# The first half of the output weights, loaded and split at a later place of the program

## The chip, the cores and the metric

One Trainium2 chip, of which the kernel uses one core. The metric is the device time of one execution in microseconds (us); lower is better. Four compute engines work beside each other, each through its own instructions in a fixed order: PE multiplies matrices, ACT (ScalarE) and DVE (VectorE) work elementwise and read PE's results, POOL (GpSimd) works elementwise on SBUF. Transfers are started by SP (most) and POOL, each again in a fixed order, and carried by 16 DMA engines that all share.

## The reference

A decoder layer on x of 1024 tokens by 1024 channels, all in float32. Cut to what matters here:

```
proj = rms_norm(x) @ w_in                      # split into q, kv, gates ...
y_a  = nsa_mixer(q, kv, ...)                   # attention: 8 heads, 3 branches
y_a  = (y_a * silu(g_nsa)) @ w_proj_a          # 512 -> 1024
y_b  = rglru_mixer(u, ...)                     # recurrent branch
y_b  = (y_b * silu(g_lru)) @ w_proj_b          # 512 -> 1024
m    = sigmoid(gate_a) * y_a + sigmoid(gate_b) * y_b
out  = x + m @ w_out                           # 1024 -> 1024
```

## The kernel before

Every float32 operand of a large product is split into a high part and a rest, and one product becomes three matmuls (`mm3`, lines 170 to 172). So each weight tile is loaded into `w_raw` (line 176; two buffers, 512 KB a load), copied to its high part on ACT, and subtracted on DVE or POOL to get the rest (lines 184, 185; for `w_out` lines 1014, 1015). A `w_raw` buffer is free again when the subtraction is done.

The program is written as a list of work, and a scheduler fixes the order on every engine when it is built: work that stands earlier in the text has precedence, work that is ready fills gaps. `attention()` writes the attention and, between its steps, pieces of the side work (`fill`). When attention is written out, the rest of the side work follows, in a tail in which all products go to the four PSUM buffers `ps_s` and all loads of a gate go to a ring of eight SBUF buffers, four cut from a tile named `bias` and four from `kTs`. The tail has these parts:

- The second branch's products with `w_pb`: eleven of them fall into the tail, each of 12 matmuls over 512 columns. A product ends with line 888 on DVE, which reads its `ps_s` buffer and a loaded gate `gb` (line 876). The result is stored to `mb` by a DMA on POOL (line 95, function `dst`), and the ring buffer is loaded again (with a gate `ga`, line 777) once that store has landed.
- `gated(1)` and `gated(0)`: the gated attention output of tokens 512 to 1023 and 0 to 511: loads of `yo` (line 761) and `gn`, lines 763 and 765 on DVE, 764 and 767 on ACT, 768 on DVE. `yo` is what attention stores (lines 709 to 711); the last of it is stored late in the tail, and two `kTs<-yo` loads wait for it.
- `merge(1)`, then `merge(0)`: eight products each with `w_pa` (four tiles), 12 matmuls a product; line 792 on DVE reads the `ps_s` buffer, then 796, 798 (ACT) and 799 make the merged tile, `big_h` or `t`.
- `out_weights(0)`, the first half of `w_out` (columns 0 to 511): four loads of 512 KB, eight ACT copies, eight DVE subtractions, into buffers that attention has given up (`p_slc`, `p_win`, `ph`, `pl`).
- The output products `ps_t` (lines 1023 on), 24 matmuls for 128 tokens by 512 columns. Those that have their merged tile and weights are put between the merge products.

A `ps_s` buffer is given to the next product only when DVE has read it, so DVE's order decides when PE may go on.

Of the kernel before, what the change touches and what calls it, by code (L numbers as in the profile page):

```python
# [73 lines left out]
def f(ap):  # L74
    return ap.bitcast(FT)


def fr(ap):
    return ap.bitcast(FR)
# [7 lines left out]
def _build(ctx, tc, A, out, dbg):  # L87
# [21 lines left out]
    @contextmanager  # L109
    def urgent(by):  # L110
        tc.cur_priority -= by
        yield
        tc.cur_priority += by
# [13 lines left out]
    def ps_f(most):  # L127

        if tail:
            return next(tail[0])()[:, 0:most]  # L130
        return (ps("ps_f", PF) if PF else ps_s())[:, 0:min(most, FW)]
# [11 lines left out]
    def ta(dt=FT):  # L143
        return K.tile([128, S], dt, name="t", bufs=NTILE)
# [4 lines left out]
    def te():  # L149
        if tail:  # L150
            return next(tail[1])
        return K.tile([128, 512], FT, name="ev", bufs=NEV)
# [4 lines left out]
    def t_st():  # L157
        return K.tile([128, 512], FT, name="st", bufs=4)
# [4 lines left out]
    def p_slc():  # L163
        return K.tile([128, 4 * WTOK], FT, name="p_slc", bufs=1)

    def p_win():
        return K.tile([128, 2560], FT, name="p_win", bufs=1)

    def mm3(o, lh, ll, rh, rl, first, last):
        T.matmul(o, lh, rh, start=first, stop=False)  # L170
        T.matmul(o, lh, rl, start=False, stop=False)  # L171
        T.matmul(o, ll, rh, start=False, stop=last)  # L172
# [354 lines left out]
    def prep_stage():  # L527
        if preps:
            try:
                next(preps[0])  # L530
            except StopIteration:
                preps.pop(0)
# [222 lines left out]
    def gated(half, y1):  # L755

        tk = slice(half * 512, (half + 1) * 512)
        ya = []
        for kc in range(4):
            yt, gt = te(), t_st()  # L760
            dma(yt, yo[2 * kc:2 * kc + 2, :, tk].rearrange("h d t -> (h d) t"))
            dma(gt, gn[kc, :, tk])
            V.scalar_tensor_tensor(out=yt, in0=yt, scalar=0.5, in1=gt, op0=OP.mult, op1=OP.mult)
            C.activation(gt, gt, AF.Tanh, scale=0.5)
            V.scalar_tensor_tensor(out=yt, in0=gt, scalar=1.0, in1=yt, op0=OP.add, op1=OP.mult)
            y2 = y1[:, kc] if y1 is not None else ta(FR)
            C.activation(y2[:, 0:512], yt, AF.Copy)
            V.tensor_tensor(out=y2[:, 512:], in0=yt, in1=f(y2[:, 0:512]), op=OP.subtract)
            ya.append(y2)
        return ya  # L770

    def merge(half, pa, m1, ya):

        tk = slice(half * 512, (half + 1) * 512)
        for m in range(8):
            gt, bt = te(), t_st()
            dma(gt, ga[m, :, tk])
            dma(bt, mb[m, :, tk])
            wh, wl = pa[m // 2]
            c = slice((m % 2) * 128, (m % 2 + 1) * 128)  # L780
            q = 0
            while q < 512:
                s = ps_f(512 - q)
                w = s.shape[-1]
                for kc in range(4):
                    mm3(s, wh[:, kc, c], wl[:, kc, c], ya[kc][:, q:q + w], ya[kc][:, 512 + q:512 + q + w],
                        kc == 0, kc == 3)
                    if kc < 3:
                        yield w * 0.00126
                tq = slice(q, q + w)  # L790
                with urgent(UPE):
                    V.scalar_tensor_tensor(out=gt[:, tq], in0=gt[:, tq], scalar=1.0, in1=s, op0=OP.add, op1=OP.mult)
                q += w
                if q < 512:
                    yield w * 0.00126
            (V if tail else G).tensor_tensor(out=gt, in0=gt, in1=bt, op=OP.add)
            mt = m1[:, m] if m1 is not None else ta(FR)
            C.activation(mt[:, 0:512], gt, AF.Copy, scale=0.5)
            V.scalar_tensor_tensor(out=mt[:, 512:], in0=gt, scalar=0.5, in1=f(mt[:, 0:512]),
                                   op0=OP.mult, op1=OP.subtract)  # L800
            mT[half, m] = mt
            yield w * 0.00126
# [111 lines left out]
    def fill(us):  # L914
        owed[0] += us
        while owed[0] > 0:
            p0 = tc.cur_priority
            tc.cur_priority = p0 + LOWP
            if LOOK and len(marks) >= LOOK:
                with tc.issue_after(marks[-LOOK]):  # L920
                    d = next(side, None)
            else:
                d = next(side, None)
            tc.cur_priority = p0 + (tc.cur_priority - p0 - LOWP if KEEPP else 0)
            if not d:
                owed[0] = 0.0
                return
            owed[0] -= d

    def attention():  # L930
        late = []

        def drain():
            if late:
                late.pop(0)()

        def prepare(*tbs):
            while any(x in tbs for x in todo):
                prep_stage()
                fill(F_PREP)  # L940

        seq = [(g,) + u for g in range(2) for u in units(g)]
        n = len(seq) // 2

        ahead = {k: [k + 1] for k in range(2 * n)}
        ahead[0] = ahead[n - 1] = []
        ahead[EARLY] += [n]
        ahead[2 * n - 1] = []
        prepare(3, 4, 5, 6, 7)
        for j in seq[0][1]():  # L950
            j()
            fill(F_Q)
        for k, (g, jobs, steps) in enumerate(seq):
            if k == n:
                drain()
                prepare(*range(NT))
            more = []
            if k == 1:
                prepare(*range(NT))
                for _ in qkv1_:  # L960
                    pass
                for j in jobs():
                    j()
                    fill(F_JOB)
                fill(F_LEAD)
            for a in ahead[k]:
                if a == n:
                    prepare(3, 4, 5, 6, 7)
                more += seq[a][1]()
            m = len(steps)  # L970
            per = (FK[k] if FK else max(F_MIN, LAT / m - 1.32)) if k else F_Q
            at = [min(m - 1, int(j * (m - 1) / max(1, len(more)))) for j in range(len(more))]
            if k > 1:
                fill(FB[k])
            for q, st in enumerate(steps):
                pvk = st()
                js = [more[j] for j in range(len(more)) if at[j] == q]
                for j in js:
                    j()
                    fill(per / len(js))  # L980
                if not js:
                    fill(per)
                drain()
                late.append(pvk)
                prep_stage()
        drain()
        wo0.extend(out_weights(0))
        r1 = K.tile([128, 4, 512], FT, name="bias")
        r2 = K.tile([128, 2, 64 + S], FT, name="kTs", bufs=1)
        ring = [r1[:, k] for k in range(4)] + [r2[:, a, c:c + 512] for a in range(2) for c in (0, 512)]  # L990
        tail.extend([itertools.cycle([ps_s] * PB[0]), itertools.cycle(ring)])
        if not pa:
            gated_y[1] = gated(1, None)
        gated_y[0] = gated(0, None)
        for _ in side:
            pass
        for _ in merge(0, pa, None, gated_y[0]):
            pass

    def out_weights(nh):  # L1000
        if nh == 0:
            ws, ww = fr(p_slc()), fr(p_win())
            wo = [(w[:, k * 1024:k * 1024 + 512], w[:, k * 1024 + 512:(k + 1) * 1024])
                  for w, n_ in ((ws, 4), (ww, 2)) for k in range(n_)]
            wo += [[K.tile([128, 512], FR, name=n_, bufs={"ph": 2, "pl": NPL}[n_]) for n_ in ("ph", "pl")] for _ in range(2)]
        else:
            w = [t_l(0, 8), t_l(1, 8)]
            wo = [(w[k // 4][:, k % 4], w[k // 4][:, 4 + k % 4]) for k in range(8)]
        for kp in range(4):
            raw = wload(A["w_out"][nh, kp])  # L1010
            for k in range(2):
                r = raw[:, k * 512:(k + 1) * 512]
                wh, wl = wo[2 * kp + k]
                C.activation(wh, r, AF.Copy)
                V.tensor_tensor(out=wl, in0=r, in1=f(wh), op=OP.subtract)
        return wo

    wo0 = []
    if True:
        attention()  # L1020
# [98 lines left out]
```

## Time and profile before

| | |
|---|---|
| median of 3 runs | 905.2 us (902.38 to 905.53) |
| the profiled execution's own time | 903.51 us |
| its span, first to last instruction | 901.7 us |
| PE busy | 872.1 us, 97% of the span |
| DVE, ACT, POOL busy | 569.1, 441.4, 298.5 us |
| DMA | 92.49 MB, mean 103 GB/s |

The profiled execution lies 1.7 us under the median. PE is busy nearly all the time, so the time is PE's work and PE's gaps. The tail runs from about 727 us to the end.

### The profile page before, as it was taken

To read this page: it belongs to the slowest core of one execution; us is meant where nothing else is said; L and a number is where in the kernel's file an instruction comes from. 1 tells how busy PE (TensorE), PEld (TensorE's weight loads), DVE (VectorE), ACT (ScalarE), POOL (GpSimd) and SP (SyncE) were. 2 spreads that over 40 slices of the span, in tenths; PEclk is the share of its full clock that TensorE was granted. 3 is DMA by queue.
4 is the path that set the end of the run, shared out by engine and by line. 5 is a ranking of instruction groups with operands and counts; after the bars stand their busy time and mean duration, and the time that the engine had idled before them with its cause. 6 is when DMAs were issued, how large, how long until landed. Compare 5 with 4: busy or idle time off the path is not lost.

```text
span 901.7 us, 15836 instructions
## 1 busy us (share of the span) xinstructions
PE 872.1 (97%) x5670; PEld 779.5 (86%) x5670; DVE 569.1 (63%) x1627; ACT 441.4 (49%) x1161; POOL 298.5 (33%) x338
## 2 busy tenths in 40 slices
PE   5999999989899999999999999999999999999998
PEld 4778888989899999999999998999998877888887
DVE  4563868897622548576577857667777886783111
ACT  7432453646423547566456757566667663331000
POOL 4032243279512435253355644233324421000000
PEclk9999999999999999999999999999999999999999
DMA  9133421202212112112122241121113369883121
GB/s 354 53 99 114 155 87 48 77 30 76 101 48 83 47 60 84 64 53 77 48 65 77 67 138 54 37 71 56 40 46 117 125 212 342 330 271 109 71 71 47
DMA packets 45519, 92.49 MB, mean 103 GB/s; under 512 B 6896, under 2 KB 12704, under 8 KB 45440
## 3 DMA queue, kind: packets, MB, share of 16 engines
q1 hardware_dynamic: 44480, 88.33, 29.3%
q0 software_dynamic: 960, 3.15, 0.9%
q8 instruction: 44, 0.72, 0.3%
q14 instruction: 35, 0.29, 0.1%
HBM read 64.15 MB, written 25.21 MB: 99 GB/s over the span
## 4 chain that ended last, share of the span: by engine, by line
PE 83%; DVE 6%; POOL 3%; DMA 3%; ACT 3%; issue 1%; SPq 0%; ACTq 0%; DVEq 0%; POOLq 0%
PE ps_f L170 10%; PE ps_f L171 9%; PE ps_f L172 9%; PE ps_s L624 7%; PE ps_s L170 7%; PE ps_s L172 7%; PE ps_s L171 7%; PE ps_t L677 6%; PE ps_t L170 4%; PE ps_t L171 4%; PE ps_t L172 4%; PE ps_o L701 3%; PE ps_o L702 3%; DVE sq L548 1%; POOL ss L193 1%
## 5 line engine op out<-in xcount | busy, mean ns | idle before, releaser
L171 PE MATMUL ps_f<-big_l,w_hi 128*128 128x256 f32 (+1 forms) x700 | 200.3, 286 | 0.0
L170 PE MATMUL ps_f<-big_h,w_hi 128*128 128x256 f32 (+1 forms) x664 | 193.8, 292 | 0.8 <-ACT ev L841 0.6
L172 PE MATMUL ps_f<-big_h,w_lo 128*128 128x256 f32 (+1 forms) x664 | 189.6, 286 | 0.0
L171 PEld LDWEIGHTS ps_f<-big_l,w_hi 128*128 128x128 f32 x700 | 131.9, 188 | 2.0
L170 PEld LDWEIGHTS ps_f<-big_h,w_hi 128*128 128x128 f32 x664 | 125.6, 189 | 4.5 <-ACT ev L841 2.0
L172 PEld LDWEIGHTS ps_f<-big_h,w_lo 128*128 128x128 f32 x664 | 125.4, 189 | 1.8 <-POOL w_lo L185 0.3
L682 DVE TENSOR_TENSOR pl<-ps_t,ph 128x512 fp32r<-128x512 f32 x132 | 90.4, 687 | 47.1 <-ACT ph L681 45.6
L185 POOL TENSOR_TENSOR w_lo<-w_raw,w_hi 128x1024 fp32r<-128x1024 f32 x32 | 77.9, 2438 | 97.6 <-ACT w_hi L184 75.0
L681 ACT ACTIVATE ph<-ps_t 128x512 fp32r<-128x512 f32 x132 | 78.1, 599 | 48.8 <-PE ps_t L677 45.5
L662 POOL TENSOR_SCALAR p_slc<-p_slc,mx,bg 128x384 f32<-128x384 f32 (+7 forms) x88 | 68.6, 785 | 90.1 <-DVE mx L661 35.3
L658 ACT ACTIVATE p_slc<-ps_s,mx 128x256 f32<-128x256 f32 (+5 forms) x128 | 68.1, 540 | 24.0 <-DVE mx L656 18.2
L171 PE MATMUL ps_s<-big_l,w_hi 128*128 128x512 f32 (+1 forms) x184 | 73.2, 398 | 0.0
L184 ACT ACTIVATE w_hi<-w_raw 128x1024 fp32r<-128x1024 f32 (+1 forms) x40 | 42.3, 1061 | 38.3 <-PE ps_f L171 17.7
L648 DVE TENSOR_REDUCE mx<-ps_s 128x1 f32<-128x256 f32 (+5 forms) x120 | 50.9, 436 | 10.7 <-PE ps_s L624 9.2
L701 PE MATMUL ps_o<-ph,t 128*128 128x512 f32 x132 | 55.7, 422 | 0.0
L170 PE MATMUL ps_s<-big_h,w_hi 128*128 128x512 f32 x136 | 54.4, 408 | 0.4 <-ACT big_h L245 0.3
L662 POOL TENSOR_SCALAR p_win<-p_win,mx,bg 128x640 f32<-128x640 f32 (+1 forms) x40 | 34.7, 869 | 59.1 <-DVE mx L661 25.0
L677 PE MATMUL ps_t<-ident_r,p_slc 128*128 128x128 f32 x336 | 54.0, 273 | 0.0
L653 DVE CUSTOM_DVE_ANT_0 ps_s<-ps_s,bias 128x256 f32<-128x256 f32 (+1 forms) x128 | 52.5, 417 | 2.3 <-POOL p_win L662 0.8
L172 PE MATMUL ps_s<-big_h,w_lo 128*128 128x512 f32 x136 | 53.4, 395 | 0.4 <-POOL w_lo L185 0.4
L624 PE MATMUL ps_s<-kTs,t 128*128 128x512 f32 (+4 forms) x224 | 53.0, 349 | 0.3 <-ACT pc L633 0.3
L702 PE MATMUL ps_o<-pl,t 128*128 128x512 f32 x132 | 53.2, 403 | 0.0
(332 smaller groups left out, 2209.9 us busy)
## 6 DMA issues: line engine op xcount, KB each, us to landing
w_raw<-in_w_in SPq DMA_DIRECT2D x30, 512.0 KB
t<-in_x SPq DMA_DIRECT2D x8, 512.0 KB
gb<-ev SPq DMA_DIRECT2D x16, 256.0 KB
ga<-ev SPq DMA_DIRECT2D x16, 256.0 KB
w_raw<-in_w_out SPq DMA_DIRECT2D x8, 512.0 KB
st<-mb SPq DMA_DIRECT2D x16, 256.0 KB
w_raw<-in_w_tok SPq DMA_DIRECT2D x6, 524.0 KB
ev<-in_cw SPq DMA_DIRECT2D x8, 256.0 KB
```

What stands on the lines that cost most here:

```text
L170: T.matmul(o, lh, rh, start=first, stop=False)
L171: T.matmul(o, lh, rl, start=False, stop=False)
L172: T.matmul(o, ll, rh, start=False, stop=last)
L185: (E or (V if tail else G)).tensor_tensor(out=lo, in0=raw, in1=f(hi), op=OP.subtract)
L624: T.matmul(s, qT[h][:, i * 128:(i + 1) * 128], rhs, start=(hl == 0), stop=(hl == 1))
L658: C.activation(p[:, h, k0:k1], sv, AF.Exp, bias=mx[:, 6:7], accum_out=mx[:, 7 + j:8 + j])
L662: G.tensor_scalar(out=p[:, h], in0=p[:, h], scalar1=mx[:, 9:10], scalar2=bg[:, g, i, 4 * (br + 1) + h:4 * (br + 1) + h + 1], op0=OP.mult, ...
L677: ins = T.transpose(pt[:, h * 128:(h + 1) * 128], p[h][:, c0:c0 + 128], ident)
L681: C.activation(ph, pt, AF.Copy)
L682: V.tensor_tensor(out=pl, in0=pt, in1=f(ph), op=OP.subtract)
L701: T.matmul(o, vf, pp[0], start=first, stop=False)
L702: T.matmul(o, vf, pp[1], start=False, stop=False)
```

## The change

The call of `out_weights(0)` moves from ahead of the ring, the gated tiles and the rest of the side work to a place behind them and ahead of `merge(0)`. Nothing is added or left out: the same four loads, eight copies, eight subtractions.

```diff
         drain()
-        wo0.extend(out_weights(0))
         r1 = K.tile([128, 4, 512], FT, name="bias")
         r2 = K.tile([128, 2, 64 + S], FT, name="kTs", bufs=1)
...
         gated_y[0] = gated(0, None)
         for _ in side:
             pass
+        wo0.extend(out_weights(0))
         for _ in merge(0, pa, None, gated_y[0]):
             pass
```

What the scheduler makes of it: until the tail, the order of every engine is as before. In the tail the four `w_pa` loads take the places of the first four `w_out` loads in the two `w_raw` buffers, and the `w_out` loads come behind. Two places follow in full.

SP's queue where the last part of `yo` is stored (`yo<-eo`) and read back (`kTs<-yo`). Before:

```order
L176 DMA w_raw_9255<-in_w_pa 128x1024
L876 DMA bias_8984<-gb_1266 128x512
L711 DMA yo_1268<-eo_8950 64x4x128
L777 DMA bias_8984<-ga_1265 128x512
L176 DMA w_raw_9261<-in_w_pa 128x1024
L777 DMA kTs_8985<-ga_1265 128x512
L761 DMA kTs_8985<-yo_1268 128x512 x2
```

And now:

```order
L876 DMA kTs_8955<-gb_1266 128x512 x2
L876 DMA bias_8954<-gb_1266 128x512
L777 DMA bias_8954<-ga_1265 128x512
L176 DMA w_raw_9237<-in_w_pa 128x1024
L711 DMA yo_1268<-eo_8950 64x4x128
L777 DMA kTs_8955<-ga_1265 128x512 x2
L761 DMA kTs_8955<-yo_1268 128x512 x2
```

Both `kTs<-gb` loads now stand behind two `bias<-gb` loads that wait for landed stores (before, one of them stood ahead of both), and the reading of `yo` now has two `kTs<-ga` loads ahead of it instead of one; each of those waits for the store of a second-branch product.

DVE's queue at the end of the second branch's products. `ps_s_9206`, `9222`, `9238` before and `ps_s_9176`, `9192`, `9208` now are the last three of them, `ps_s_9279` and `ps_s_9249` the first merge product. Before:

```order
L888 SCALAR_TENSOR_TENSOR bias_8984<-bias_8984,ps_s_9206 128x512
L185 TENSOR_TENSOR w_lo_9258<-w_raw_9255,w_hi_9257 128x1024
L888 SCALAR_TENSOR_TENSOR bias_8984<-bias_8984,ps_s_9222 128x512
L888 SCALAR_TENSOR_TENSOR bias_8984<-bias_8984,ps_s_9238 128x512
L185 TENSOR_TENSOR w_lo_9264<-w_raw_9261,w_hi_9263 128x1024
L763 SCALAR_TENSOR_TENSOR kTs_8985<-kTs_8985,st_9040 128x512
L792 SCALAR_TENSOR_TENSOR bias_8984<-bias_8984,ps_s_9279 128x512
```

And now:

```order
L888 SCALAR_TENSOR_TENSOR bias_8954<-bias_8954,ps_s_9192 128x512
L763 SCALAR_TENSOR_TENSOR kTs_8955<-kTs_8955,st_9010 128x512
L763 SCALAR_TENSOR_TENSOR kTs_8955<-kTs_8955,st_9019 128x512
L765 SCALAR_TENSOR_TENSOR kTs_8955<-st_9010,kTs_8955 128x512
L888 SCALAR_TENSOR_TENSOR bias_8954<-bias_8954,ps_s_9208 128x512
L765 SCALAR_TENSOR_TENSOR kTs_8955<-st_9019,kTs_8955 128x512
L185 TENSOR_TENSOR w_lo_9234<-w_raw_9231,w_hi_9233 128x1024
L185 TENSOR_TENSOR big_l1_9224<-w_raw_9237,big_l1_9224 128x1024
L768 TENSOR_TENSOR t_9016<-kTs_8955,t_9016 128x512
L792 SCALAR_TENSOR_TENSOR bias_8954<-bias_8954,ps_s_9249 128x512
```

Before, line 888 of the last second-branch product stood ahead of the two lines 763, which wait for the read of `yo`; now it stands behind them. By the waits in the built program, the second merge product gets its `ps_s` buffer from that line 888, and the third from line 792 of the first, which now has both `w_pa` subtractions ahead of it.

## Rows read from the trace of the kernel before

**Rows 1.** The page: PE's busy time, and its granted clock in 40 slices.

```profile
PE 872.1 (97%) x5670; PEld 779.5 (86%) x5670; DVE 569.1 (63%) x1627; ACT 441.4 (49%) x1161; POOL 298.5 (33%) x338
...
PEclk9999999999999999999999999999999999999999
```

**Rows 2.** Windows of 3 us: busy time by engine, PE clock, DMA share, GB/s.

```profile
723.00:726.00 3.00, 2.56 (x19) 2.05 (x17) 1.99 (x8) 1.50 (x11) 1.43 (x2) 1.00 0.68 203
...
747.00:750.00 3.00, 1.66 (x7) 1.05 (x6) 3.00 (x6) 0.77 (x2) 0.71 (x2) 1.00 1.01 383
...
777.00:780.00 3.00, 3.00 (x14) 2.42 (x13) 2.30 (x4) 1.65 (x3) 0.00 (x0) 1.00 1.05 401
```

**Rows 3.** Timeline of PE: start us, us, instruction [idle before <-releaser].

```profile
747.25 0.40 PE L172 MATMUL ps_s<-big_l,w_lo 128*128 128x512 f32 x1
748.99 0.50 PE L170 MATMUL ps_s<-big_l,w_hi 128*128 128x512 f32 x1 [1.34 <-DVE bias L888]
...
757.40 0.40 PE L172 MATMUL ps_s<-big_l,w_lo 128*128 128x512 f32 x1
758.39 0.50 PE L170 MATMUL ps_s<-big_l,w_hi 128*128 128x512 f32 x1 [0.60 <-DVE kTs L888]
...
764.05 0.39 PE L170 MATMUL ps_s<-t,w_hi 128*128 128x512 f32 x1
...
777.50 0.39 PE L170 MATMUL ps_s<-t,big_l 128*128 128x512 f32 x1
...
790.55 0.39 PE L170 MATMUL ps_s<-t,w_hi 128*128 128x512 f32 x1
```

**Rows 4.** Timeline of DVE.

```profile
730.81 0.69 DVE L763 SCALAR_TENSOR_TENSOR bias<-bias,st 128x512 f32<-128x512 f32 x1 [2.15 <-DMA bias<-yo]
...
743.54 0.68 DVE L888 SCALAR_TENSOR_TENSOR bias<-bias,ps_s 128x512 f32<-128x512 f32 x1
...
747.05 1.29 DVE L1015 TENSOR_TENSOR p_slc<-w_raw,p_slc 128x512 fp32r<-128x512 f32 x2
748.26 1.28 DVE L888 SCALAR_TENSOR_TENSOR bias<-bias,ps_s 128x512 f32<-128x512 f32 x2
...
766.40 1.23 DVE L185 TENSOR_TENSOR w_lo<-w_raw,w_hi 128x1024 fp32r<-128x1024 f32 x1 [1.46 <-ACT w_hi L184]
767.54 0.69 DVE L763 SCALAR_TENSOR_TENSOR kTs<-kTs,st 128x512 f32<-128x512 f32 x1
```

**Rows 5.** Timeline of ACT, splits that waited for their load.

```profile
755.54 0.63 ACT L1014 ACTIVATE ph<-w_raw 128x512 fp32r<-128x512 f32 x1 [2.53 <-DMA w_raw<-in_w_out]
...
765.30 1.06 ACT L184 ACTIVATE w_hi<-w_raw 128x1024 fp32r<-128x1024 f32 x1 [6.05 <-DMA w_raw<-in_w_pa]
...
782.69 1.16 ACT L1014 ACTIVATE big_l<-w_raw 128x512 fp32r<-128x512 f32 x2 [2.67 <-DMA w_raw<-in_w_out]
```

**Rows 6.** Timeline of SP: start of an issue, and its length.

```profile
726.64 1.92 SPq L761 DMA_DIRECT2D bias<-yo  x4
...
748.37 0.33 SPq L176 DMA_DIRECT2D w_raw<-in_w_out  x1
750.00 0.32 SPq L876 DMA_DIRECT2D bias<-gb  x1
...
757.65 0.58 SPq L711 DMA_DIRECT2D yo<-eo  x1
...
758.98 0.38 SPq L176 DMA_DIRECT2D w_raw<-in_w_pa  x1
...
760.24 2.35 SPq L761 DMA_DIRECT2D kTs<-yo  x2
...
777.74 0.33 SPq L176 DMA_DIRECT2D w_raw<-in_w_out  x1
```

**Rows 7.** POOL's timeline, one store of `mb`; then DMA issues, 700 to 830 us.

```profile
744.52 0.54 POOL L95 DMA_DIRECT2D mb<-bias  x1 [2.44 <-DVE bias L888]
...
mb<-kTs POOLq DMA_DIRECT2D x4, 256.0 KB, 4.1
```

## The prediction

> **What bounds the kernel now.** I read the page first: PE is busy 872.1 us, 97% of the span, at a granted clock of nine tenths or more in every slice [rows 1]. So the time is PE's work, which the change leaves alone, and PE's gaps, of which it can add or take some. Until the tail the order is as before, so I went to the tail. Its windows show DVE full from 747 to 750 us, and a DMA share near 1.0 there and at 777 [rows 2]. PE's timeline shows what that costs: behind the attention's last steps PE waits only twice. At 748.99 it has idled 1.34 us for a line 888 on a ring buffer `bias`, and at 758.39 it has idled 0.60 us for a line 888 on `kTs` [rows 3]. A matmul of these products takes 0.232 us (58 of them from 764.05 to 777.50 [rows 3]), so a product of twelve takes 2.78. A matmul that starts at 747.25 should be followed at 747.48 and is followed at 748.99: 1.51 us lost. From 757.40 to 758.39 it is 0.76. Together 2.27 us.
>
> Both have to do with the first `w_out` half. The first line 888, at 748.26, stands behind two line 1015 (747.05 to 748.26, so 0.60 us an operation [rows 4]). Ahead of the second, DVE has a line 1015 that waits for ACT's line 1014, and ACT waits 2.53 us, until 755.54, for a `w_out` load [rows 5].
>
> **What the change removes.** Ahead of both places no line 1015 is left. If nothing new came, the first merge product m0 (764.05 before) would start at 764.05 - 2.27 = 761.78. The work moved costs no time of its own elsewhere: the four loads, eight copies and eight subtractions stand later beside the merge products, where ACT and DVE have room between operations (DVE is busy 2.30 and ACT 1.65 of 3 us at 777 [rows 2]).
>
> **What it adds.** Three waits, each read from the two orders and priced by rows of before. For a flight (issue to landing) I have these: a `yo` load 4.2 us (issued at 726.64 [rows 6], its first user at 730.81 [rows 4]); `w_out` 7.2 (748.37 [rows 6] to 755.54 [rows 5]) and 4.9 (777.74 to 782.69); `w_pa` 6.3 (758.98 to 765.30); the `mb` store of a `bias` buffer 5.5 (744.52 [rows 7] to 750.00, when the load behind it could be issued [rows 6]), of a `kTs` buffer 4.1 in the median [rows 7]; the `yo` store 2.6 (757.65 to 760.24, when its reading was issued [rows 6]). I take the row of the same transfer where there is one.
>
> *First wait.* SP's two `kTs<-gb` loads now stand behind a `bias<-gb` load that waits for a landed `mb` store. The line 888 which that store follows ran to 744.2 before (743.54 and 0.68 [rows 4]), with two line 1015 ahead of it since 739.9 that are gone now, so it ends by 743.0 to 744.2. I take 743.6. Store issued at 744.0, landed at 749.5, the two `kTs<-gb` loads issued at 749.9 and 750.3, landed 4.2 later at 754.1 and 754.5, their lines 888 done at 754.7 and 755.3. The third last second-branch product gets its `ps_s` buffer from the first of these. Without a wait it would start three products ahead of m0, at 761.78 - 8.34 = 753.4. It starts at 754.75: **+1.35**. m0 then starts at 763.1, and m1 could start at 765.9.
>
> *Second wait.* m1 gets its buffer from line 888 of the last second-branch product, and that now stands behind both lines 763, which need `yo` read back. The reading stands on SP behind two `kTs<-ga` loads, each waiting for a store of a `kTs` product: line 888 done at 755.3, store issued at 755.7, landed at 759.8; two loads issued, 0.4 each; reading issued at 760.6, landed at 764.8. (The `yo` store itself, which now stands behind a `w_pa` load, goes out at about 757.1 and lands at 759.7: just not the last.) Then two lines 763 to 766.0, a line 765 to 766.6, line 888 to 767.2. m1 starts at 767.3: **+1.4**.
>
> *Third wait.* m2 gets its buffer from line 792 of m0, with a line 765, two line 185 (1.14 each, 766.40 to 767.54 [rows 4]) and a line 768 ahead of it on DVE: 767.8, 768.95, 770.1, 770.7, and 792 done at 771.3. m1 ends at 770.1, so m2 starts at 771.4: **+1.3**. Queued behind it: m3 follows from 774.2 to 777.0. m4 needs line 792 of m2, which stands behind the last `w_pa` split: buffer free at 768.95, load issued at 769.1, landed at 774.0 (4.9), ACT 1.05, line 185 1.14, then 799 and 792, done at 777.4. So m4 starts at 777.5, as before [rows 3], but by then before had also done ten matmuls of output products between m2 and m4 (58 less 48), and now only some two fit. 8 x 0.232 = 1.86: the same lag as the sum.
>
> The `w_out` splits, late now, are needed by the first output products behind m4. Four loads of 4.9 to 7.2 us with two buffers end by about 788, and output products give way to merge products until then, so I cost this at nothing; without that cover it would be a wait of up to one flight, 4.9 to 7.2, and is counted to the slower rival. merge(0) starts at 790.55 before [rows 3].
>
> **Sum.** +1.35 + 1.4 + 1.3 - 2.27 = **+1.8 us**; merge(0) at 792.4. On the profiled execution's own 903.51 that is 905.3. That execution lies 1.7 under the median 905.2, so the predicted median is **907.0**.
>
> **Bounds.** Everything hangs on when `yo` has been read back (x = 764.8 here), since from there the chain to m2 is fixed DVE work. The saving is all spent when x is 764.8 - 1.8 = 763.0. Below: with all flights at 2.6, the shortest row, x is near 758 and no new wait remains, -2.3. Above: with `gb` and `yo` loads and the last `w_pa` load at 6.3 to 7.2, as in rows of the same queue [rows 5, 6], x goes up by 2 x 2.1 to 2 x 3.0 and the split of the last `w_pa` by 1.4 more, so up to +1.8 + 5.7 = +7.5. I took 4.2, since a `yo` load in an emptier stretch took it (DMA share 0.68 at 723 [rows 2]), and the stretch of 747 to 765 loses 2 MB of `w_out` loads by this change.
>
> The Trainium skill, "DMA: Bandwidth & Descriptors", section "Anatomy of one DMA — SWDGE (gpsimd) path", gives a transfer a fixed cost of about 2.0 us plus its bytes at 436 GB/s. By it 256 KB take an estimated 2.6 us, and the case without new waits would follow. Only the `yo` store agrees (2.6); the `mb` store of the same size took 5.5 and the `yo` load 4.2, and the measurement decides.
>
> **The rivals.**
>
> *Gain only.* The two gaps go and DMAs, with less to carry, land in time. For it: four 512 KB loads leave the full stretch. Against it: the waits on stores are chains of two to three flights, and each must shrink by a third. It needs x under 760.8: without gaps m2 would start at 769.60 - 2.27 = 767.3, and DVE's chain from x to that line 792 is 6.5 us. Time: 905.2 - 2.3 = 902.9.
>
> *Slower.* The transfers stay as long as the longest rows, because the `w_pa` loads take the places of the `w_out` loads and the DMA share stays at 1.0 [rows 2]. It decides when the flights of `gb`, `yo` and the last `w_pa` together are more than 2.7 us above mine (4.5 us is 0.5% of 905.2, about what a measurement of this kernel can tell from no change, less 1.8). Price: +4.5 to +7.5, 909.7 to 912.7, middle 911.
>
> *PE's clock falls.* New gaps could cost more than their length. At 1.2 GHz instead of 2.4 a product would take 2.78 us more, so three at that clock +8.3: 915. Against it: the granted clock stands at 1.00 in the window behind the gap of 1.34 us, and at nine or more in all slices [rows 1, 2].
>
> The Trainium skill, "TensorE: Matmul & The Clock Gate", section "HAM oscillation — how this bites in real kernels", warns that idle gaps let the clock drop to half. This trace, with its gap of 1.34 us, shows no drop.
>
> **How the numbers follow.** Forecast, new waits as priced: 0.45 (same). Gain only: 0.25 (same, as 2.3 is under 4.5). Slower by long flights: 0.25. Clock: 0.02 (slower). More than 4.5 us gained: 0.03, since the tail's gaps sum to 2.27. So faster 0.03, same 0.70, slower 0.27. The likeliest is 907.0. The range reaches down to gain only, 902.7, and up to 911.5 within the longest flights; above lies about one in ten.
>
> **What would show each step.** Right: no gap near 747 and 757; a gap of 1.4 us three products ahead of m0, released by line 888 on `kTs`; m1 delayed 1.4 us by line 888 on `bias`, and the first line 763 of `kTs` on DVE at about 764.8 after a wait for `kTs<-yo`; m2 delayed 1.3 us by line 792; `kTs<-yo` issued at about 760.6; the first output product behind m3; merge(0) at 792.4; clock 1.00 throughout. Wrong: line 763 ahead of 761, or behind 768; gaps behind m4 released by ACT's line 1014 or a `w_out` load; any gap ahead of 725, where nothing should differ.

## The result: 5 us slower, in three new waits

The changed kernel takes 909.35 us in the median (908.86 to 910.68, 4 runs), the kernel before 904.27 beside it (902.38 to 905.53, 4 runs): a ratio of 1.0063, with a 95% interval of 1.0042 to 1.0083. Of 5.1 us, 1.8 were forecast.

The profiled execution's span is 907.3 us, 5.6 above that of before. Part of it lies ahead of the tail, where nothing differs. So I count from a mark in PE's row that the change doesn't touch, its last wait of the attention (line 658, 1.91 us in both). PE's timeline of before has it at 727.47; the other two rows are its m1 and m2:

```profile
727.47 0.39 PE L170 MATMUL ps_s<-big_l,w_hi 128*128 128x256 f32 x1 [1.91 <-ACT p_slc L658]
...
766.83 0.39 PE L170 MATMUL ps_s<-t,w_hi 128*128 128x512 f32 x1
...
769.60 0.40 PE L170 MATMUL ps_s<-t,w_hi 128*128 128x512 f32 x1
```

PE's timeline of the changed kernel has it at 728.91. The rows behind it are the third last second-branch product, m0, m1, m2, and the first product of merge(0):

```profile
728.91 0.39 PE L170 MATMUL ps_s<-big_l,w_hi 128*128 128x256 f32 x1 [1.91 <-ACT p_slc L658]
...
754.45 0.40 PE L172 MATMUL ps_s<-big_l,w_lo 128*128 128x512 f32 x1
756.11 0.50 PE L170 MATMUL ps_s<-big_l,w_hi 128*128 128x512 f32 x1 [1.26 <-DVE kTs L888]
...
764.54 0.39 PE L170 MATMUL ps_s<-t,w_hi 128*128 128x512 f32 x1
...
767.08 0.39 PE L172 MATMUL ps_s<-t,w_lo 128*128 128x512 f32 x1
770.76 0.50 PE L170 MATMUL ps_s<-t,w_hi 128*128 128x512 f32 x1 [3.30 <-DVE bias L888]
...
773.42 0.40 PE L172 MATMUL ps_s<-t,w_lo 128*128 128x512 f32 x1
774.93 0.47 PE L170 MATMUL ps_s<-t,w_hi 128*128 128x512 f32 x1 [1.11 <-DVE bias L792]
...
796.03 0.40 PE L170 MATMUL ps_s<-t,w_hi 128*128 128x512 f32 x1
```

The two gaps of before [rows 3] are gone, and the three forecast ones stand at their places with the forecast releasers. With 0.232 from a matmul's start to the next one's, they lose 756.11 - 754.68 = 1.43, 770.76 - 767.31 = 3.45, and 774.93 - 773.65 = 1.28 us. The table has each product's start behind the mark, less that of before (m0 36.58, m1 39.36, m2 42.13, merge(0) 63.08, from these rows and [rows 3] less 727.47). The last two columns are two further profiles of the same kernel (the fifth and the twelfth experiment, marks at 727.55 and 725.88).

| | forecast | profile 1 | profile 2 | profile 3 |
|---|---|---|---|---|
| m0 | -0.95 | -0.95 | -0.92 | -0.56 |
| m1 | +0.47 | +2.49 | +2.55 | +2.89 |
| m2 | +1.80 | +3.89 | +5.06 | +4.57 |
| merge(0) | +1.85 | +4.04 | +5.67 | +4.72 |

The mean of merge(0) over the three, +4.8, agrees with the 5.1 of the medians. Up to m0 the forecast's time holds to 0.4 us (in profile 2 by another way, see the fifth experiment); between m0 and m1 it is 2 us short. DVE and SP show why. DVE's timeline of the changed kernel, from the first gap to the third:

```profile
755.37 1.35 DVE L888 SCALAR_TENSOR_TENSOR kTs<-kTs,ps_s 128x512 f32<-128x512 f32 x2 [5.95 <-DMA kTs<-gb]
...
767.62 0.69 DVE L763 SCALAR_TENSOR_TENSOR kTs<-kTs,st 128x512 f32<-128x512 f32 x1 [4.97 <-DMA kTs<-yo]
768.82 0.69 DVE L763 SCALAR_TENSOR_TENSOR kTs<-kTs,st 128x512 f32<-128x512 f32 x1 [0.51 <-DMA kTs<-yo]
...
770.03 0.68 DVE L888 SCALAR_TENSOR_TENSOR bias<-bias,ps_s 128x512 f32<-128x512 f32 x1
...
771.23 1.22 DVE L185 TENSOR_TENSOR w_lo<-w_raw,w_hi 128x1024 fp32r<-128x1024 f32 x1
...
774.10 0.68 DVE L792 SCALAR_TENSOR_TENSOR bias<-bias,ps_s 128x512 f32<-128x512 f32 x1
```

SP's timeline of the same kernel:

```profile
748.94 1.28 SPq L876 DMA_DIRECT2D kTs<-gb  x2
...
757.87 0.33 SPq L176 DMA_DIRECT2D w_raw<-in_w_pa  x1
758.60 0.58 SPq L711 DMA_DIRECT2D yo<-eo  x1
759.27 3.73 SPq L777 DMA_DIRECT2D kTs<-ga  x2
763.75 0.86 SPq L761 DMA_DIRECT2D kTs<-yo  x2
```

In the kernel before, the last `w_pa` load ahead of that `yo` store (757.65 [rows 6]) had gone out here:

```profile
753.84 0.33 SPq L176 DMA_DIRECT2D w_raw<-in_w_pa  x1
```

Line 888 of the last second-branch product stands ready on PE's side when its product has ended (764.5) and runs at 770.03, behind the two lines 763 that wait for `yo`. The `yo` store went out at 758.60, 757.16 on the clock of before (1.44 less), as forecast (757.1). But its reading was issued at 763.75, 762.31 on that clock, where 760.6 was forecast. The second `kTs<-ga` load had gone out by 763.0; the last 0.7 us ahead of 763.75 SP waited for the landing of the `yo` store.

### The profile page after: what moved, and what is told of

Same layout as the page of the kernel before. It is cut to its first block, busy times and chain, and to the rows that moved or that the text cites. A ratio compares the mean times of both kernels' runs of the same rounds, so it can differ in the third digit from the quotient of the medians.

```text
span 907.3 us, 15842 instructions
## 1 busy us (share of the span) xinstructions
PE 873.4 (96%) x5670; PEld 780.0 (86%) x5670; DVE 569.3 (63%) x1627; ACT 441.6 (49%) x1161; POOL 298.4 (33%) x338
## 4 chain that ended last, share of the span: by engine, by line
PE 81%; DVE 7%; DMA 4%; POOL 3%; ACT 2%; issue 2%; SPq 1%; DVEq 0%; POOLq 0%; ACTq 0%
PE ps_f L170 9%; PE ps_f L171 9%; PE ps_f L172 9%; PE ps_s L624 7%; PE ps_s L170 7%; PE ps_s L171 6%; PE ps_s L172 6%; PE ps_t L677 6%; PE ps_t L170 4%; PE ps_t L172 4%; PE ps_t L171 4%; PE ps_o L701 3%; PE ps_o L702 3%; DVE sq L548 1%; POOL ss L193 1%
```

## The experiments

Twelve runs. Beside them the kernel before took 903.59 us in the first four, 903.64 in the second four, 904.64 in the ninth and tenth, and 903.60 in the last two (medians of 11 to 29 runs). My theory: the chain through `yo`, with DVE's order, makes the loss. Its rivals: full DMA engines, the late `w_out` half itself, PE's clock.

**1. The reading of `yo` ahead of the two `kTs<-ga` loads on SP.**

```diff
-            dma(yt, yo[2 * kc:2 * kc + 2, :, tk].rearrange("h d t -> (h d) t"))
+            yo_read[half] = dma(yt, yo[2 * kc:2 * kc + 2, :, tk].rearrange("h d t -> (h d) t")).ins
...
-            dma(gt, ga[m, :, tk])
+            with tc.issue_after(yo_read[0]) if half and m in (1, 2) else ExitStack(): dma(gt, ga[m, :, tk])
```

> The changed kernel, with two loads held back on SP: the two kTs<-ga loads of the first merge stand behind the reading of yo, not ahead of it. If the big loss (3.45 us ahead of the second merge product m1) comes from the reading of yo standing behind two loads that wait for stores: yo is read when its own store has landed, issued at 761.2 to 762.0 in place of 763.75; m1's wait falls by 1.8 to 2.6 us, the other two gaps (1.43 and 1.28 lost) stay; about 907 in place of 909.35. Rival, the transfers are long because the DMA engines are full: the reading is issued sooner but lands no sooner, m1's wait stays near 3.4, 909. Rival, the w_out splits behind m4 are what costs: nothing changes, 909.

906.85 us (906.50 to 907.58), ratio 1.0043 (1.0027 to 1.0058). SP's timeline:

```profile
756.68 0.33 SPq L176 DMA_DIRECT2D w_raw<-in_w_pa  x1
757.41 0.58 SPq L711 DMA_DIRECT2D yo<-eo  x1
761.40 0.79 SPq L761 DMA_DIRECT2D kTs<-yo  x2
```

Now nothing stands between the two on SP, and the reading still comes 3.99 us behind the store. m1's idle time falls to 2.05 us (768.32, mark at 727.58), so m1 comes 1.1 us sooner than in profile 1, not 1.8 to 2.6. The `ga` loads are one part of the wait, and the `yo` store's own flight the larger one.

**2. The splits of two `w_pa` tiles on POOL, off DVE.**

```diff
-            pa.append(wtile(A["w_pa"][t], 4, into))
+            pa.append(wtile(A["w_pa"][t], 4, into, G if t in (1, 2) else None))
```

> The changed kernel, with the subtractions of the second and third w_pa tile on POOL. If m2 waits because two line 185 (2.27 us together) stand ahead of line 792 of m0 on DVE: the 1.28 us lost ahead of m2 go, 908.0 in place of 909.35; the waits ahead of the third last second-branch product (1.43) and of m1 (3.45) stay. Rival, m2 then waits for POOL's own subtraction of its weights (2.4 us an operation, POOL against 1.14 on DVE): a wait of up to 1 us is left, released by POOL, 909.

911.81 us (910.38 to 913.24), ratio 1.0091 (1.0071 to 1.0112): worse than both. The timeline of DVE and POOL behind m1:

```profile
771.88 2.39 POOL L185 TENSOR_TENSOR w_lo<-w_raw,w_hi 128x1024 fp32r<-128x1024 f32 x1
772.68 4.47 DVE L768 TENSOR_TENSOR t<-kTs,t 128x512 fp32r<-128x512 f32 x1 [1.04 <-ACT t L767]
774.22 2.38 POOL L185 TENSOR_TENSOR big_l<-w_raw,big_l 128x1024 fp32r<-128x1024 f32 x1
777.07 0.67 DVE L792 SCALAR_TENSOR_TENSOR bias<-bias,ps_s 128x512 f32<-128x512 f32 x1
```

DVE's line 768 takes 4.47 us where it takes 0.68 elsewhere; it ends 0.55 us behind POOL's second subtraction (777.15 and 776.60). Line 792 of m0 comes as late as ever. So neither account of m2's wait was tested here: POOL's subtractions held DVE up. PE's clock fell too (0.66, 0.50 and 0.57 in the 3 us windows behind its three gaps, at 756, 771 and 777).

**3. gated(0) behind the side work, the change otherwise kept.**

```diff
-        gated_y[0] = gated(0, None)
         for _ in side:
             pass
+        gated_y[0] = gated(0, None)
         wo0.extend(out_weights(0))
```

> The changed kernel, with gated(0) written behind the rest of the side work instead of ahead of it, so that its loads and lines 763 to 768 have the lower precedence. If the three waits all hang on the chain through yo: none of the three gaps is left (1.43 + 3.45 + 1.28 = 6.2), 903.2. Rival, the late w_out splits cost something themselves: 905 to 907, with gaps behind m4 that ACT's line 1014 or DVE's line 1015 releases. Rival, gated(0) comes too late for the second merge: a new gap ahead of merge(0), up to some us.

903.76 us (902.18 to 907.04, 10 runs), ratio 1.0006 (0.9993 to 1.0019): the whole loss is gone, and all three gaps. The gaps of the tail that are left, in PE's timeline:

```profile
789.83 0.50 PE L170 MATMUL ps_t<-p_win,big_h 128*128 128x512 f32 x1 [0.90 <-ACT big_h L798]
...
795.53 0.74 PE L172 MATMUL ps_t<-ph,big_h 128*128 128x512 f32 x2 [1.03 <-DVE big_h L799]
```

The three waits hang on gated(0)'s place. Output products now wait 1.93 us for merged tiles, so 1.93 of the 6.2 us come back, in a place that no theory had named: released by lines 798 and 799, not by a `w_out` split.

**4. The kernel before, with the `w_out` splits on POOL.**

```diff
-                V.tensor_tensor(out=wl, in0=r, in1=f(wh), op=OP.subtract)
+                (V if nh else G).tensor_tensor(out=wl, in0=r, in1=f(wh), op=OP.subtract)
```

> The kernel before, with the eight subtractions of the first w_out half on POOL instead of DVE. If DVE's line 1015 is what made the two gaps of the kernel before (1.51 and 0.76): both go, 904.3 - 2.3 = 902.0. Rival: POOL also issues the mb stores, and now waits for the w_out loads ahead of them, so stores and the gates loaded behind them come later: the gaps come back as waits for DVE's line 888 or 792, 904 to 907.

907.20 us (904.92 to 910.06), ratio 1.0039 (1.0021 to 1.0058). PE's gaps in the tail:

```profile
750.71 0.40 PE L172 MATMUL ps_s<-big_l,w_lo 128*128 128x512 f32 x1
751.37 0.51 PE L170 MATMUL ps_s<-big_l,w_hi 128*128 128x512 f32 x1 [0.26 <-DVE bias L888]
...
761.39 0.50 PE L170 MATMUL ps_s<-big_l,w_hi 128*128 128x512 f32 x1 [1.20 <-DVE kTs L888]
...
773.83 0.47 PE L170 MATMUL ps_s<-t,w_hi 128*128 128x512 f32 x1 [1.08 <-ACT t L767]
```

The first gap of before shrinks from 1.34 to 0.26, but not because line 888 comes sooner. The mark lies at 729.37 here, and the granted clock behind it is 0.52 from 730 to 733, so PE reaches the place 1.56 us later than before (21.57 us behind the mark, not 20.01). It goes on at 22.00, 0.48 later than before (21.52). Ahead of that line 888, a line 765 on DVE takes 1.78 us in place of 0.69 while POOL subtracts. So this run can't tell what line 1015 on DVE cost. The second gap grows from 0.60 to 1.20 and a third comes. The time is that of the rival, but the way is another. DVE's timeline ahead of the first and the second gap, then ACT's:

```profile
747.23 1.78 DVE L765 SCALAR_TENSOR_TENSOR kTs<-st,kTs 128x512 f32<-128x512 f32 x1
...
759.93 0.69 DVE L710 TENSOR_TENSOR eo<-ps_o,eo 64x512 f32<-64x512 f32 x1 [4.05 <-ACT eo L709]
760.65 0.69 DVE L888 SCALAR_TENSOR_TENSOR kTs<-kTs,ps_s 128x512 f32<-128x512 f32 x1
```

```profile
758.65 0.63 ACT L1014 ACTIVATE ph<-w_raw 128x512 fp32r<-128x512 f32 x1 [4.36 <-DMA w_raw<-in_w_out]
759.30 0.59 ACT L709 ACTIVATE eo<-ps_o 64x512 f32<-64x512 f32 x1
```

The `w_out` load landed at 758.65; ACT's row waited for it, and DVE's line 888 behind ACT's line 709. So the second gap is one of the load, whichever engine subtracts.

**5 and 12. The changed kernel again.**

> The changed kernel itself, profiled once more. The theory (three waits on the chain through yo, 6.2 us lost, less the 2.27 of before that are gone, +3.9 to +4.2 in the tail) says the same three gaps at the same places, with sizes that hang on the flights: 3.0 to 4.0 us idle ahead of m1 if yo is read as late as in the first profile. If PE's clock takes part, some executions show a granted clock of 0.5 for some us behind one of these gaps, and those are 2 to 3 us longer. 908 to 910 in all.

> The changed kernel once more, as the partner of the eleventh experiment on the same chip: 908 to 910, ratio to the kernel before 1.0055; the executions at a mean clock of 0.992 are some 2 us above those at 0.996 that lost nothing ahead of the tail.

909.28 us (908.88 to 909.39), ratio 1.0057 (1.0044 to 1.0069), and 908.16 us (906.71 to 910.39), ratio 1.0052 (1.0035 to 1.0068). Both profiles repeat the wait ahead of m1 (3.31 and 3.27 us idle, the same releaser). Of the other two, the twelfth has the first (1.68 us idle) and the fifth has neither. In the fifth the granted clock had already fallen behind the mark (0.62 and 0.81 from 727 to 733), so PE came to the place of the first wait when its buffer was free: m0's -0.92 in the table is the forecast's number, but not its wait. The fifth also shows what the `ga` loads do. Its reading of `yo` goes out 33.83 us behind the mark, as in the first experiment (33.82), but with both `ga` loads right ahead of it, and its first line 763 starts 1.2 us later (38.85 and 37.61). New is the clock. The windows of the fifth experiment's profile (busy time of PE, PEld, DVE, ACT, POOL; granted clock; DMA share; GB/s):

```profile
765.00:768.00 3.00, 1.14 (x5) 0.58 (x4) 1.33 (x2) 0.55 (x2) 0.00 (x0) 1.00 0.66 255
768.00:771.00 3.00, 1.54 (x4) 1.25 (x5) 2.89 (x4) 3.00 (x6) 0.54 (x1) 0.61 0.31 87
771.00:774.00 3.00, 3.00 (x9) 2.32 (x8) 3.00 (x6) 0.53 (x2) 0.00 (x0) 0.50 1.05 297
774.00:777.00 3.00, 3.00 (x12) 2.38 (x11) 2.06 (x4) 0.00 (x0) 0.00 (x0) 0.75 0.83 294
```

Behind the wait, PE runs at the lower of its two levels until about 775: m1 takes 769.46 to 774.74, 5.28 us, in place of 2.89 in profile 1. The third wait then vanishes, as line 792 of m0 is done by 773.5. So by m2 the drop costs 2.39 less 1.28. The twelfth shows the same, shorter (0.61 and 0.82 from 768 to 774); profile 1 shows 1.00 throughout the tail. Of the 15 executions of the changed kernel, 12 had a mean clock under 0.996; of the 73 of the kernel before beside the experiments, 16. The 2 to 3 us that this should cost show in the twelfth (908.59 to 910.39 at a mean of 0.992, 906.71 at 0.998) and not in the fifth (909.28 and 909.39 at 0.992, 909.01 at 0.998).

**6. The kernel before with gated(0) behind the side work, `w_out` ahead of all.**

```diff
-        gated_y[0] = gated(0, None)
         for _ in side:
             pass
+        gated_y[0] = gated(0, None)
```

> The kernel before (w_out ahead) with gated(0) written behind the side work: the same move as in the third experiment, without the change of this case. It tells what the change is worth where the chain through yo is out of the way. If the late w_out has a gain of its own (2.3 us, DVE free of line 1015 among the second branch's products): this kernel keeps the gaps of before near 747 and 757 and takes 903.6, and the third experiment should have been at 901.3 but for its 1.9 us of new gaps. Rival, the gaps of before came from DVE's load of both w_out and gated(0): they go here too, 901.3 to 902.

902.44 us (900.50 to 904.58, 12 runs), ratio 0.9984 (0.9975 to 0.9994): 1.2 us under the kernel before. PE is busy 164.94 of the 165 us from 728 to 893 (windows of that profile, columns as above):

```profile
747.00:750.00 3.00, 3.00 (x15) 2.40 (x14) 1.77 (x4) 1.54 (x3) 0.00 (x1) 1.00 0.99 348
...
780.00:800.00 20.00, 20.00 (x87) 16.13 (x86) 16.69 (x28) 8.41 (x14) 0.00 (x0) 1.00 0.86 280
```

In 747 to 750 DVE is busy 1.77 of 3 us, not 3.00 [rows 2]. The gaps of before go when the `w_out` half moves (the change) and when gated(0) moves (here), so they came from both together. And the late `w_out` half shows no gain of its own: where the chain through `yo` is out of the way, the kernel with the half ahead (902.44) is no slower than those with the half behind (903.76, and 902.89 in the seventh).

**7. The changed kernel, with gated(0) behind the `w_out` half too.**

```diff
-        gated_y[0] = gated(0, None)
         for _ in side:
             pass
         wo0.extend(out_weights(0))
+        gated_y[0] = gated(0, None)
```

> The changed kernel with gated(0) behind the side work and behind the w_out half too. If the 1.9 us of new gaps in the third experiment (output products waiting for lines 798 and 799) came from gated(0) taking DVE and ACT ahead of them: they go, 901.7 to 902. Rival, they came from line 1015 ahead of lines 796 and 799 on DVE: they stay, 903.8. Rival, gated(0) is late for merge(0): a gap there, above 904.

902.89 us (901.06 to 905.87, 12 runs), ratio 0.9995 (0.9983 to 1.0008). One gap behind m4 is left in PE's timeline, 0.58 us in place of 1.93, so gated(0) had made most of it:

```profile
794.01 0.73 PE L172 MATMUL ps_t<-ph,big_h 128*128 128x512 f32 x2 [0.58 <-DVE big_h L799]
```

**8. SP's order changed at both places.** The edit of the first, and

```diff
...
-                    dma(g_, gb[m, :, tk])
+                    with tc.issue_after(gb_load[5]) if len(gb_load) > 7 else ExitStack(): ld = dma(g_, gb[m, :, tk]).ins; gb_load.extend([ld] if tail else [])
```

> The changed kernel with SP's order changed at both places: the two kTs<-gb loads ahead of the bias<-gb loads that wait for landed stores, and the reading of yo ahead of the two kTs<-ga loads. If SP's order sets the first two waits: the kTs<-gb loads go out when line 768 has freed their buffers, some 1.0 us sooner, the first wait falls from 1.43 to about 0.4, yo is stored and read 1 us sooner than in the first experiment; m1 starts 2.2 us sooner than in the changed kernel, m2 2.3: 907.0 in place of 909.35, no more, since the yo store's own flight (4.0 us in the first experiment) is then what is left. Rival, full DMA engines: no gain beyond the first experiment's 906.85.

907.37 us (905.72 to 909.85, 10 runs), ratio 1.0037 (1.0025 to 1.0048). In the profile the size holds: m2 starts 43.72 us behind the mark (771.95 and 728.23), 2.3 sooner than in profile 1. The medians can't tell this kernel from the first experiment's (ratio 1.0043), which is what the rival said. The place of the wait is another than forecast. DVE's timeline:

```profile
764.41 0.69 DVE L763 SCALAR_TENSOR_TENSOR kTs<-kTs,st 128x512 f32<-128x512 f32 x1 [6.75 <-DMA kTs<-yo]
765.02 0.68 DVE L888 SCALAR_TENSOR_TENSOR bias<-bias,ps_s 128x512 f32<-128x512 f32 x1
```

The scheduler put a line 763 ahead of the last but one line 888 as well, so now m0 waits 3.37 us for it, and m1 doesn't. The wait follows line 763 in DVE's row.

**10. Half of the change.** Two `w_out` loads with their splits stay where they were, two come late.

```diff
         drain()
-        wo0.extend(out_weights(0))
+        wo0.extend(out_weights(0, range(0, 2)))
...
+        out_weights(0, range(2, 4), wo0)
...
-        for kp in range(4):
+        for kp in kps:
```

> Half of the change: the first two w_out loads with their splits stay ahead of the ring, the last two stand ahead of merge(0). In the order built so, all lines 888 of the second branch's bias products stand ahead of the two lines 763 on DVE, as before, and four line 1015 stay among them. If the loss comes from DVE's order (last line 888 behind lines 763 that wait for yo): the 3.45 us ahead of m1 are gone though two w_out loads come late; the gap at 747 of before (1.51) stays, that at 757 goes (0.76): 902.9, at most 904. Rival, late w_out loads and splits cost by themselves: halfway between both kernels, 906.4.

906.27 us (902.75 to 908.74, 12 runs), ratio 1.0017 (1.0003 to 1.0031). PE's gaps in the tail:

```profile
748.63 0.50 PE L170 MATMUL ps_s<-big_l,w_hi 128*128 128x512 f32 x1 [0.95 <-DVE bias L888]
...
770.11 0.47 PE L170 MATMUL ps_s<-t,w_hi 128*128 128x512 f32 x1 [1.51 <-ACT t L767]
```

The wait ahead of m1 is gone, as DVE's order said (line 888 at 763.04, line 763 at 765.20). The gap near 748 shrinks from 1.34 to 0.95 with half of the `w_out` splits in place. The wait ahead of m2 (770.11) I had not counted: line 792 of m0 still stands behind both lines 763 and both `w_pa` splits and ends at 769.97 (the view names ACT's line 767, which ends 0.06 later and makes a tile of gated(0)). By the time alone the rival fits better: its 906.4 is a ratio of 1.0024, within the interval, and 904 is 0.9997, outside. But the profiled execution took 904.08, and its two gaps cost 0.5 us more than those of before; no gap in it is released by a `w_out` load or split. What the other executions lost stays open (6 of the 12 had a mean clock under 0.996).

**9 and 11. The wait ahead of m1 filled with matmuls.** Twelve more matmuls whose result nobody reads; in the eleventh the output products are held behind m4 too.

```diff
...
+            if (half, m) == (1, 0):
+                d = ps_o()
+                with tc.issue_after(m0_last):
+                    for kc in range(4):
+                        mm3(d, wh[:, kc, c], wl[:, kc, c], ya[kc][:, 0:512], ya[kc][:, 512:1024], kc == 0, kc == 3)
...
                     for kc in range(8):
+                      with tc.issue_after(m_last[1, 4]):
```

The last added line is that of the eleventh.

> The changed kernel with twelve more matmuls (m0's own operands, into a ps_o buffer that nobody reads) between m0 and m1 on PE, where PE is idle 3.3 us in both profiles of the changed kernel. They take 2.78 us at full clock and fit in the wait. If the length of the gap alone is what is lost, and the clock has no part: nothing changes, 909.3. If some executions of the changed kernel lose 2 to 3 us more because the clock falls behind this long idle stretch (granted 0.50 from 770 to 775 in the second profile): those losses go, mean clock 0.996 in most executions in place of 0.992, 906.5 to 908. Rival, the extra work is in the way (m1 could have started sooner): above 909.3.

> As the ninth experiment (twelve more matmuls in the wait between m0 and m1), and the output products are held behind m4 on PE, so that none of them waits for a late w_out split. If only the length of the gap is lost and the clock has no part: the same as the changed kernel beside it. If the clock falls behind the 3.3 us of idle in some executions of the changed kernel: none of these shows a granted clock of 0.5 behind m0, the mean clock is 0.995 or more in most, and the median is 1 to 3 us below the changed kernel's. Rival: PE meets another late buffer and waits elsewhere, at or above the changed kernel.

912.96 us (912.70 to 914.29), ratio 1.0100 (1.0083 to 1.0117), and 912.90 us (910.43 to 914.16), ratio 1.0096 (1.0079 to 1.0113). Both came out as their rivals said, above the changed kernel, and both are inconclusive on the clock. It is 1.00 from 768 to 777 in both profiles, behind the filled wait, but so it was in profile 1; it falls behind the later 2.42 and 4.89 us (0.50 from 780 to 783). The extra work fits the wait (m1 starts 41.77 and 41.21 us behind the mark, 41.85 in profile 1), but the order of what comes behind is another than in the changed kernel. PE's timeline of the ninth, then of the eleventh (their line numbers are 1 to 6 higher behind the edit):

```profile
769.59 0.50 PE L170 MATMUL ps_s<-t,w_hi 128*128 128x512 f32 x1 [0.74 <-DVE bias L894]
...
779.20 1.22 PE L170 MATMUL ps_t<-p_slc,big_h 128*128 128x512 f32 x2 [2.42 <-ACT p_slc L1020]
```

```profile
780.36 0.79 PE L170 MATMUL ps_s<-t,w_hi 128*128 128x512 f32 x1 [4.89 <-DVE kTs L793]
```

In the ninth an output product comes too early for its `w_out` split, the wait that the prediction costed at nothing where its cover holds; in the eleventh a merge product waits 4.89 us for a `ps_s` buffer.

## Why the prediction was right in kind and short in size

- **What is removed (-2.27).** Right: both gaps gone, m0 0.95 earlier behind the mark after the first wait, as forecast. Why they were there was only half right: the change itself and the sixth experiment show the `w_out` half and gated(0) sharing the blame.
- **First wait (+1.35).** Right in the place and the releaser, and by luck in the size, 1.43. The two flights behind it were off in opposite ways: the `kTs<-gb` loads went out at 748.94 - 1.44 = 747.5, not 749.9, and took 6.4 us (748.94 to 755.37), not 4.2. In profile 2 the wait isn't there.
- **Second wait (+1.4, measured 3.45).** The mis-sized term. The forecast let the `yo` store land 2.6 us after its issue, "just not the last". In the first experiment, with nothing between, it is 3.99 us, and in the fifth 4.13 (757.25 to 761.38). In profile 1 it is 5.15 (758.60 to 763.75), and it was the last after all. So the reading went out 1.7 us late (762.31 against 760.6). It landed 0.3 sooner than forecast, and the chain behind it was 0.6 longer: 3.14 us from the first line 763 to m1 against 2.5, as the second read landed 1.2 us behind the first. 1.7 - 0.3 + 0.6 = 2.0 is the whole difference of 3.45 - 1.4.
- **Why the `yo` store took longer.** The 2.6 was read rightly for before: in the packets of the kept traces, the store's 256 packets of 512 bytes end at 759.71 there, 0.53 ahead of the reading, and 0.43 to 0.50 ahead of it in profile 1 and the first and fifth experiments. What had changed is the place in SP's queue. Before, the last `w_pa` load had gone out 3.81 us ahead of the store (753.84 and 757.65); in the changed kernel it goes out 0.73 ahead (757.87 and 758.60). All 128 of that load's packets of 4 KB then start behind the store's issue and ahead of its last packet; before, 1 such packet did. The fourth experiment, with the load 4.23 ahead, has 2.52 again; eight profiles with the load 0.7 ahead have 3.82 to 5.15, and the tenth, 1.96 ahead, 4.58. The prediction saw that the store "now stands behind a `w_pa` load" and still took the row of before for its flight. No run moves that load alone, so the cause is read from the traces and not isolated. (The prediction also set the 2.6 beside an estimate for 256 KB; the store moves 128 KB.)
- **Third wait (+1.3).** 1.28 in profile 1. It is hidden where the clock falls (profiles 2 and 3).
- **`w_out` late, at nothing.** Right in the changed kernel: no gap behind m4 in profile 1. The ninth experiment shows it without its cover, 2.42 us.
- **The rivals.** Gain only fell: no part of the saving was left by m1. That the DMAs would have less to carry was wrong, the share stayed near full ahead of the first wait (0.97 in 747 to 753), as the slower rival had it. The measured 5.1 us even lies in that rival's +4.5 to +7.5, but not by its way: of its three loads `gb` took 2.2 us more than mine, `yo` 0.3 less and the last `w_pa` the same (772.48 to 777.43 in profile 1), together 1.9 and not the 2.7 that it needed. (Its upper bound is also added up wrong: 2 x 3.0 and 1.4 on top of 1.8 make +9.2, not +7.5.) PE's clock was given 0.02, since one gap of 1.34 us showed no drop; it fell behind m1's wait in two of three profiles. Its price is not the 8.3 us of that rival, since it is short and a slow m1 hides the third wait: from m1 to merge(0), profiles 2 and 3 lose 1.6 and 0.3 us more than profile 1.

Here the Trainium skill, "TensorE: Matmul & The Clock Gate", section "HAM oscillation — how this bites in real kernels", warned of this: idle gaps can let the clock fall to half. Profiles 2 and 3 agree (0.50 and 0.61 behind m1's wait), profile 1 does not (1.00).

## What to carry to other kernels

Work that fills an engine's row also holds other work back. Taking it away lets the scheduler bring forward an instruction that waits for a transfer (here line 763), and everything behind it in that in-order row waits too. So ask which instruction moves up into the place, and what it waits for. That work is needed late doesn't tell that it should be written late: the `w_out` half is, and moving it back lost 5 us. Moving gated(0), whose input lands late, gave the gain that was there (902.44 against 903.64). And price a transfer by what stands ahead of it in its queue: the same `yo` store took 2.6 us in one place and 3.8 to 5.2 in another.

## What the runs showed of the hardware that was not expected

The same idle time is followed by different clocks. Behind the 1.91 us at line 658, the window from 727 to 730 has a granted clock of 1.00 in the kernel before and 0.62 in the fifth experiment; behind the 3.3 us ahead of m1 it stays at 1.00 in profile 1 and falls to 0.50 in profile 2. So one profile without a drop doesn't exclude it, and what decides it stays open.

POOL can hold DVE up: line 768, with two operands in SBUF, took 4.47 us beside two POOL subtractions (second experiment) and 0.68 alone; line 765 took 1.78 beside POOL and 0.69 without (fourth experiment and before). The Trainium skill, "SBUF — State Buffer", section "Who interferes with whom", says that a DVE instruction with two SBUF inputs contends with a GpSimd instruction that reads SBUF, and these traces agree. In the tail, splits on POOL cost time in both runs that tried them (911.81 and 907.20).
